# Gated recurrent heads in pairs on the free axis, and the level of 64 spread over both column halves

## The chip, the cores and the metric

The kernel runs on one core of a Trainium2 chip. The metric is the time of one execution on the device, in microseconds (us); lower is better. The core's engines are TensorE (PE in the profile; PEld is its weight load), VectorE (DVE), ScalarE (ACT), GpSimd (POOL) and SyncE (SP, whose queue issues most DMAs).

## The reference, cut to what matters

The program is three layers on a sequence of S = 512 positions and D = 1024 channels: first a block with its own mixers and a feed-forward part (`first_block`), then two layers of `hybrid_layer`. The change concerns the recurrence in those two, `hgrn2`: 8 heads of width 128, in chunks.

```python
def hgrn2(q, f_logit, i, lb):
    # S_t = diag(f_t) S_{t-1} + (1 - f_t) i_t^T,  o_t = S_t^T q_t
    ...
    qf = silu(q)
    logf = logaddexp(log(max(lb, LB_FLOOR)), log1p(-lb) + log_sigmoid(f_logit))
    k = -expm1(logf)
    ...
    def step(state, xs):
        qch, kch, vch, b = xs          # b = cumulative sum of logf in the chunk
        decay = exp(b_t - b_s) for s <= t, else 0
        scores = einsum('bhtd,bhsd,bhtsd->bhts', qch, kch, decay)
        o = scores @ vch + (qch * exp(b)) @ state
        state = exp(b_last) * state + (kch * exp(b_last - b))^T @ vch
        return state, o

def hybrid_layer(x, w_in, w_out, g_pre, g_post, lb, g_head, sinks):
    proj = rms_norm(x, g_pre) @ w_in
    q_h, f_h, i_h, z_h, q_a, k_a, v_a, z_a = split(proj)
    o_h = rms_norm(hgrn2(q_h, f_h, i_h, lb), g_head) * silu(z_h)
    o_a = sliding_window_attention(rotary(q_a), rotary(k_a), v_a, sinks) * silu(z_a)
    return x + rms_norm(concat(o_h, o_a) @ w_out, g_post)
```

## The kernel before, in words

**Order of the work.** The code is written with a scheduler that places each instruction on its engine's queue by a priority: without more, the order of the text. `K.above(mark)` gives a piece of code a priority above what follows the mark, `EVP` puts the copies out of the accumulators ahead of these, and `prio=20000` the splitting of weights ahead of all. The queue of each engine is fixed when the program is built; on the chip each engine goes through its own queue in order.

**Projections.** `gemm_a` and `gemm_b` multiply the layer's input with 512 columns of weights. Each float32 product is made from three (L149, L150, L151): both operands are split into a high and a low part, ACT casting the high part of the weights (L137) and DVE subtracting (L138). Eight row blocks times three make 24 matmuls for one accumulator `mm`, of which there are two. A callback `evac` takes the accumulator out.

**Tags.** A tile is asked for by a tag with so many buffers; a new tile of that tag waits until the one before it in its buffer has had its last reader. `ev` (4) holds what the evacuations need for a short time: the sigmoid in `proj_q`, `proj_zh` and `proj_za`, two tiles of the rotary evacuation (`rope`, L522 to L524), and one more in `turn` of `proj_kv`. `ha` (4) and `hb` (4) serve the attention, `f` (4) the gates, `zs` (2) the output gates read back. In the accumulator memory (PSUM) the tags `xa` and `xb` have two banks each, `xc` one; heads and attention share them.

**A head** (`hgrn`, L413 to L511) takes three 128x512 tiles with the head's 128 channels on the partitions and time on the free axis: q, k and the decay f. It builds the masked score matrix from the diagonal outwards in 7 levels, b = 1, 2, 4, ... 64. At each level PE multiplies blocks of k with blocks of q, and DVE's masked copies (L435, L436, L445, L452) or ACT's copies (L456, L465, L471) put the part that belongs to this level into a matrix `C` and then `ST`. Then DVE scales (L478, L479) the later half of q's blocks and the earlier half of k's by the decay products of the neighbouring block, which are in T, and multiplies neighbours in T (L481) to get the products for blocks twice as long. So a level's matmuls need the scaling of the level before, and overwriting q and k needs the matmuls of the level.

The matmuls of a level contract over all 128 partitions. Up to b = 32 they have 32 columns of weights, and `pa[32 * j:32 * j + 32, ...]` puts the outputs on four groups of 32 rows in turn (at b = 32 two groups): 16, 16, 16, 16, 16, 8 matmuls. At b = 64 there are four with 64 columns of weights, all on rows 0 to 63:

```python
for c in range(NT):
    o = c * P
    nc.tensor.matmul(pb[0:64, 64 * c:64 * c + 64], k[:, o:o + 64], q[:, o + 64:o + 128])
nc.scalar.copy(ST[0:64, :, 64:128], pb[0:64, 0:256].rearrange("p (c t) -> p c t", c=4))
```

Level 1 reads q through a copy `qx` (L421, L423) of 16 blocks of 48 columns. Levels b = 1, 2, 4 use the bank `pa` (tag `xa`), the others `pb` (tag `xb`). After the levels the head transposes k (L486), forms the states of the chunks (L490 to L494), and the output from `ST` and the states (L498, L500), normalises it (L504 to L510) and multiplies it with its output gate, all through the one bank of `xc`.

**The layer** runs projections of the first four heads (`proj_i`, `proj_q`, `proj_f`), then heads 0 to 3 with priority over the next projections, `proj_kv`, `proj_zh`, `proj_qa`, `proj_za`, then heads 4 to 7 in the same way, then the attention in eight `swa_pair` calls, whose last ones have the first half of the output projection (`wo1`) behind them; `wo2` needs all attention results. Two layers of 8 heads are 16 heads.

Of the kernel before, what the change touches and what calls it, by code (L numbers as in the profile page):

```python
# [8 lines left out]
F32 = mybir.dt.float32  # L9
# [3 lines left out]
AF = mybir.ActivationFunctionType  # L13
ALU = mybir.AluOpType
# [3 lines left out]
P = 128  # L18
S = 512
D = 1024  # L20
NT = S // P
KT = D // P
EPS = 1e-6
# [295 lines left out]
def layer(K, l, xd, win, wout, gpost, lbp, ghead, sinks, out, gnext):  # L319

    nc, tc = K.nc, K.tc
    if True:
        def page(tag, bufs):
            return K.lp.tile([P, S], F32, name=K.nm("pg"), tag=tag, bufs=bufs)

        def ev():
            return page("ev", 4)

        def ha():
            return page("ha", 4)  # L330

        def hb():
            return page("hb", 4)
# [36 lines left out]
        def proj_q(c):  # L370
            quad = K.quad()

            def evac(m, ps):
                h = 4 * c + m
                sg = ev()
                nc.scalar.activation(sg, ps, AF.Sigmoid)
                q = quad[:, m, :]
                nc.vector.scalar_tensor_tensor(q, ps, om[:, h:h + 1], sg, ALU.mult, ALU.mult)
                qh[h] = q
            K.gemm_a(win[:, c * S:(c + 1) * S], evac)  # L380

        def proj_f(c):
            quad = K.quad()

            def evac(m, ps):
                h = 4 * c + m
                k, f = quad[:, m, :], page("f", 4)
# [3 lines left out]
                fh[h] = (f, k)  # L391
            K.gemm_a(win[:, D + c * S:D + (c + 1) * S], evac)
# [20 lines left out]
        def hgrn(h):  # L413
            q, (f, k) = qh.pop(h), fh.pop(h)
            v = vh[h // 4]
            vc = slice((h % 4) * P, (h % 4 + 1) * P)
            ST, C = K.STs[h % 2], K.Cs[h % 2]
            zs = page("zs", 2).rearrange("p (c d) -> p c d", c=NT)
            nc.sync.dma_start(out=zs, in_=zh_d[:, h * P:(h + 1) * P].rearrange("(c p) d -> p c d", p=P))
            qx = K.lp.tile([P, 16, 48], F32, name=K.nm("qx"), tag="qx", bufs=1)  # L420
            nc.scalar.copy(qx[:, :, 0:32], q.rearrange("p (n t) -> p n t", n=16))  # L421
            nc.vector.tensor_tensor(q, q, f, ALU.mult)
            nc.scalar.copy(qx[:, :, 32:48], q.rearrange("p (n t two) -> p n t two", n=16, two=2)[:, :, :, 1])  # L423
            pa, pb = K.psum("xa"), K.psum("xb")
            T, b = f, 1
            Cf = C.rearrange("p c t -> p (c t)")
            for lev in range(7):
                if b == 1:
                    for c in range(NT):
                        for j in range(4):  # L430
                            o = c * P + 32 * j
                            nc.tensor.matmul(pa[32 * j:32 * j + 32, 48 * c:48 * c + 48], k[:, o:o + 32], qx[:, 4 * c + j, :])
                    p1 = pa[:, 0:192].rearrange("p (c t) -> p c t", c=NT)
                    m1 = K.hgmask[:, 0:192]
                    nc.vector.copy_predicated(C, m1[:, 0:P].rearrange("p (c t) -> p c t", c=NT), p1[:, :, 0:32])  # L435
                    nc.vector.copy_predicated(C.rearrange("p c (t two) -> p c t two", two=2)[:, :, :, 1],  # L436
                                              m1[:, P:192].rearrange("p (c t) -> p c t", c=NT), p1[:, :, 32:48])
                elif b <= 8:
                    pl, o0 = (pb, 320) if b == 8 else (pa, 64 + P * lev)
                    for c in range(NT):  # L440
                        for j in range(4):
                            o = c * P + 32 * j
                            nc.tensor.matmul(pl[32 * j:32 * j + 32, o0 + 32 * c:o0 + 32 * c + 32],
                                             k[:, o:o + 32], q[:, o:o + 32])
                    nc.vector.copy_predicated(Cf, K.hgmask[:, 64 + P * lev:64 + P * (lev + 1)], pl[:, o0:o0 + P])  # L445
                elif b == 16:
                    for c in range(NT):
                        for j in range(4):
                            o = c * P + 32 * j
                            nc.tensor.matmul(pb[32 * j:32 * j + 32, 256 + 16 * c:272 + 16 * c],  # L450
                                             k[:, o:o + 32], q[:, o + 16:o + 32])
                    nc.vector.copy_predicated(C[:, :, 16:32], K.hgmask[:, 576:640].rearrange("p (c t) -> p c t", c=4),  # L452
                                              pb[:, 256:320].rearrange("p (c t) -> p c t", c=4))
                    for j in range(4):
                        r = slice(32 * j, 32 * j + 32)
                        nc.scalar.copy(ST[r, :, r], C[r, :, :])  # L456
                elif b == 32:
                    for c in range(NT):
                        for j in range(2):
                            o = c * P + 64 * j  # L460
                            nc.tensor.matmul(pb[64 + 32 * j:96 + 32 * j, 32 * c:32 * c + 32],
                                             k[:, o:o + 32], q[:, o + 32:o + 64])
                    for j in range(2):
                        r = slice(64 * j, 64 * j + 32)
                        nc.scalar.copy(ST[r, :, 64 * j + 32:64 * j + 64],  # L465
                                       pb[64 + 32 * j:96 + 32 * j, 0:P].rearrange("p (c t) -> p c t", c=4))
                else:
                    for c in range(NT):
                        o = c * P
                        nc.tensor.matmul(pb[0:64, 64 * c:64 * c + 64], k[:, o:o + 64], q[:, o + 64:o + 128])  # L470
                    nc.scalar.copy(ST[0:64, :, 64:128], pb[0:64, 0:256].rearrange("p (c t) -> p c t", c=4))  # L471
                n = S // (2 * b)
# [7 lines left out]
                T2 = K.lc.tile([P, n], F32, name=K.nm("T"), tag=f"T{n}", bufs=1 if n >= 128 else 2)  # L480
                nc.vector.tensor_tensor(T2, T4[:, :, 0], T4[:, :, 1], ALU.mult)  # L481
                T, b = T2, 2 * b
            pk = K.psum("xc", 1).rearrange("p (c d) -> p c d", c=NT)
            kt = hb().rearrange("p (c d) -> p c d", c=NT)
            for c in range(NT - 1):
                nc.tensor.transpose(pk[:, c, :], k[:, c * P:(c + 1) * P], K.ident)  # L486
            nc.scalar.copy(kt[:, 0:3, :], pk[:, 0:3, :])
            pS = K.psum("xc", 1).rearrange("p (c d) -> p c d", c=NT)
            for c in range(NT - 1):
                nc.tensor.matmul(pS[:, c, :], kt[:, c, :], v[c][:, vc])  # L490
            Ss = hb().rearrange("p (c d) -> p c d", c=NT)
            nc.vector.tensor_copy(Ss[:, 0, :], pS[:, 0, :])
            for c in range(1, NT - 1):
                nc.vector.scalar_tensor_tensor(Ss[:, c, :], Ss[:, c - 1, :], T[:, c:c + 1], pS[:, c, :],  # L494
                                               ALU.mult, ALU.add)
            po = K.psum("xc", 1).rearrange("p (c d) -> p c d", c=NT)
            for c in range(NT):
                nc.tensor.matmul(po[:, c, :], ST[:, c, :], v[c][:, vc], start=True, stop=(c == 0))  # L498
                if c:
                    nc.tensor.matmul(po[:, c, :], q[:, c * P:(c + 1) * P], Ss[:, c - 1, :], start=False, stop=True)  # L500
            o = page("on", 8).rearrange("p (c d) -> p c d", c=NT)
            ss = K.small(NT, "hss", 4)
            for c in range(NT):
                nc.scalar.activation(kt[:, c, :], po[:, c, :], AF.Square, accum_out=ss[:, c:c + 1])  # L504
            nc.vector.tensor_tensor(o, po, zs, ALU.mult)
            ms = K.small(NT, "hms", 4)
            nc.vector.tensor_scalar(ms, ss, 1.0 / P, EPS, ALU.mult, ALU.add)  # L507
            rs = K.rsqrt(ms)
            for c in range(NT):
                nc.vector.tensor_scalar(o[:, c, :], o[:, c, :], rs[:, c:c + 1], None, ALU.mult)  # L510
            on[h] = o  # L511
# [69 lines left out]
        oa = [page("f", 4) for _ in range(4)] + [page("on", 8) for _ in range(4)]  # L581
# [70 lines left out]
        with K.above(p0):  # L652
            for h in range(4):
                hgrn(h)
# [4 lines left out]
        with K.above(p1):  # L659
            for h in range(4, 8):  # L660
                hgrn(h)
# [606 lines left out]
```

## Time and profile before

| | |
|---|---|
| runs | 1810.46, 1810.53 and 2941.12 us, median 1810.53 us |
| profiled execution | 1814.22 us, span of its instructions 1812.5 us |
| granted TensorE clock, mean | 0.993 |
| PE busy | 98% of the span |
| DVE busy, ACT busy, POOL busy | 60%, 48%, 10% |
| instructions on PE, DVE | 11600, 2186 |

Busy is the time in which at least one instruction of the engine is under way; matmuls overlap, and their ends are modelled, so that 98% is an upper reading of how full PE is. Start times count from the span's start. The two layers with heads run from about 840 to 1338 us and from there to the end.

### The profile page before, as it was taken

How to read it: one execution, taken by the hardware profiler on the slowest of the kernel's cores; microseconds unless marked ns; L12 is line 12 of the kernel's file. 1: busy time of each engine (PE TensorE's matmuls, PEld its weight loads, DVE VectorE, ACT ScalarE, POOL GpSimd, SP SyncE). 2: the span in 40 equal slices, each digit the busy share in tenths (PEclk: the TensorE clock that was granted, in tenths of full speed). 3: DMA queues.
4: the chain of work that ended last, by engine and by line, in shares of the span. 5: the costliest groups of instructions: out<-in, count | busy, mean ns of one | idle time of the engine just before them, and what ended most of it. 6: DMA issues, size and time to landing. Idle time of an engine off the chain costs nothing.

```text
span 1812.5 us, 29438 instructions
## 1 busy us (share of the span) xinstructions
PE 1775.7 (98%) x11600; PEld 1460.7 (81%) x11600; DVE 1080.5 (60%) x2186; ACT 864.0 (48%) x1707; POOL 172.6 (10%) x231
## 2 busy tenths in 40 slices
PE   7999999999899999999999999999999999999998
PEld 5878887787698888878888888878878888888886
DVE  4375445557455665588474666766364748577744
ACT  4457744344343443445443445766343334376741
POOL 1001111010000110012000001100120000111002
PEclk9999999999999999999999999999999999999999
DMA  7342433121623847388322233332342322332222
GB/s 211 75 109 80 90 93 93 47 93 47 197 94 101 236 114 189 94 205 235 109 88 84 88 100 100 100 110 82 108 154 88 112 76 65 119 127 76 82 70 93
DMA packets 114322, 201.05 MB, mean 111 GB/s; under 512 B 9600, under 2 KB 20224, under 8 KB 114184
## 3 DMA queue, kind: packets, MB, share of 16 engines
q1 hardware_dynamic: 105480, 182.40, 32.6%
q0 software_dynamic: 8704, 16.78, 5.3%
q8 instruction: 91, 1.49, 0.3%
q14 instruction: 47, 0.39, 0.1%
HBM read 184.45 MB, written 14.70 MB: 110 GB/s over the span
## 4 chain that ended last, share of the span: by engine, by line
PE 92%; DMA 3%; ACT 2%; DVE 1%; issue 1%; POOL 0%; SPq 0%; DVEq 0%; POOLq 0%; ACTq 0%
PE mm L150 23%; PE mm L151 23%; PE mm L149 23%; PE xc L638 2%; PE xa L602 2%; PE xa L228 2%; PE xa L227 2%; PE xa L229 2%; PE mm L227 1%; PE mm L228 1%; PE mm L229 1%; PE xc L1069 1%; PE xa L1051 1%; PE xb L624 1%; PE xc L498 1%; DMA wr<-in_w_in_dram 1%
## 5 line engine op out<-in xcount | busy, mean ns | idle before, releaser
L149 PE MATMUL mm<-wh,hh 128*128 128x512 f32 (+1 forms) x896 | 350.0, 391 | 9.5 <-ACT hh L258 3.7
L138 DVE TENSOR_TENSOR wl<-wr,wh 128x1024 fp32r<-128x1024 f32 (+1 forms) x240 | 288.5, 1211 | 114.4 <-PE mm L150 70.8
L150 PE MATMUL mm<-wl,hh 128*128 128x512 f32 (+1 forms) x896 | 350.0, 391 | 0.8 <-DVE wl L138 0.8
L151 PE MATMUL mm<-wh,hl 128*128 128x512 f32 (+1 forms) x896 | 349.1, 393 | 0.0
L137 ACT CAST wh<-wr 128x1024 fp32r<-128x1024 f32 (+1 forms) x240 | 246.6, 1038 | 118.6 <-PE mm L151 55.3
L149 PE MATMUL mm<-hh,wh 128*128 128x512 f32 x640 | 253.6, 396 | 1.4 <-ACT pg L803 1.4
L151 PE MATMUL mm<-hh,wl 128*128 128x512 f32 x640 | 252.3, 394 | 2.1 <-DVE wl L138 2.0
L150 PE MATMUL mm<-hl,wh 128*128 128x512 f32 x640 | 252.3, 394 | 0.0
L149 PEld LDWEIGHTS mm<-wh,hh 128*128 128x128 f32 x896 | 170.5, 190 | 43.6 <-ACT hh L258 4.3
L150 PEld LDWEIGHTS mm<-wl,hh 128*128 128x128 f32 x896 | 170.4, 190 | 34.7 <-DVE wl L138 2.4
L151 PEld LDWEIGHTS mm<-wh,hl 128*128 128x128 f32 x896 | 169.1, 190 | 31.5 <-DVE hl L259 0.5
L151 PEld LDWEIGHTS mm<-hh,wl 128*128 128x128 f32 x640 | 120.3, 188 | 28.4 <-DVE wl L138 3.3
L149 PEld LDWEIGHTS mm<-hh,wh 128*128 128x128 f32 x640 | 120.2, 188 | 28.1 <-ACT pg L803 2.7
L150 PEld LDWEIGHTS mm<-hl,wh 128*128 128x128 f32 x640 | 120.4, 188 | 24.5 <-issue 0.2
L115 POOL TENSOR_TENSOR sm<-sm,nhalf 128x4 f32<-128x4 f32 (+1 forms) x64 | 59.0, 922 | 491.6 <-DVE sm L507 331.4
L149 PE MATMUL mm<-qd,wh 128*128 128x512 f32 (+1 forms) x288 | 105.5, 366 | 0.0
L150 PE MATMUL mm<-qd,wh 128*128 128x512 f32 (+1 forms) x288 | 105.4, 366 | 0.0
L151 PE MATMUL mm<-qd,wl 128*128 128x512 f32 (+1 forms) x288 | 105.2, 365 | 0.0
L610 ACT ACTIVATE pg<-pg,sm 128x256 f32<-128x256 f32 (+1 forms) x128 | 60.9, 478 | 11.0 <-DVE sm L608 10.6
L1151 DVE TENSOR_TENSOR hr<-hr 128x512 f32<-128x512 f32 (+1 forms) x36 | 22.7, 631 | 69.4 <-ACT hr L1150 68.8
L151 PEld LDWEIGHTS mm<-qd,wl 128*128 128x128 f32 x288 | 54.3, 189 | 8.8
L149 PEld LDWEIGHTS mm<-qd,wh 128*128 128x128 f32 x288 | 54.3, 189 | 8.8
(311 smaller groups left out, 2996.9 us busy)
## 6 DMA issues: line engine op xcount, KB each, us to landing
wr<-in_w_in_dram SPq DMA_DIRECT2D x160, 512.0 KB, 4.9
wr<-in_w_out_dram SPq DMA_DIRECT2D x40, 512.0 KB, 3.5
wr<-in_w_up_dram SPq DMA_DIRECT2D x32, 512.0 KB, 5.7
wr<-in_w_down_dram SPq DMA_DIRECT2D x32, 512.0 KB, 5.9
wx<-in_w_down_dram POOLq DMA_DIRECT2D x24, 512.0 KB, 9.5
wx<-in_w_down_dram SPq DMA_DIRECT2D x8, 512.0 KB, 3.5
wr<-in_w_down_dram POOLq DMA_DIRECT2D x8, 512.0 KB, 8.4
zh<-pg SPq DMA_DIRECT2D x16, 256.0 KB, 2.5
```

What stands on the lines that cost most here:

```text
L115: self.nc.gpsimd.tensor_tensor(y, ms, e, ALU.pow)
L137: nc.scalar.copy(hi, raw)
L138: nc.vector.tensor_tensor(lo, raw, hi.bitcast(F32), ALU.subtract)
L149: nc.tensor.matmul(ps, sh, mh, start=(k == 0), stop=False)
L150: nc.tensor.matmul(ps, sh, ml, start=False, stop=False)
L151: nc.tensor.matmul(ps, sl, mh, start=False, stop=(k == n - 1))
L227: nc.tensor.matmul(ps, ah, wh, start=(first and k == 0), **kw)
L228: nc.tensor.matmul(ps, ah, wl, start=False, **kw)
L229: nc.tensor.matmul(ps, al, wh, start=False, **kw)
L602: nc.tensor.matmul(psc[:, i, 2 * P - wi:], qT[p][e][:, t1 - P:t1], kT[kv][j][:, t1 - wi:t1], start=(j == 0), stop=(j == 1))
L610: nc.scalar.activation(prw, prw, AF.Exp, bias=pn[:, n:n + 1], scale=-1.0, accum_out=den[:, n:n + 1])
L638: nc.tensor.matmul(o, va[0][:, k, vv], pTs[e][k // 2][:, k % 2, w], start=(k == n), stop=(k < n or n == 0))
```

## The change

`hgrn(h)` becomes `hgrn2(i)` for heads 2i and 2i + 1. Their q, k and f lie side by side in 1024 columns, so that one DVE instruction scales both; matmuls, masked copies and everything after the levels are still done for each head (`for e in range(2)`), with both heads' matmuls of a level ahead of both heads' copies. A pair takes two banks of `xa` and two of `xb`. The first decay product, now of 512 columns, is a tile of tag `ev`; `f` is two tiles of 1024 columns (`f2`), `ha` too (`ha2`, handed out in halves by `ha`), and `qx` uses `ha2`. The smaller decay products have one buffer each. At b = 64 the four matmuls of a head go to rows 0 to 63 and 64 to 127 in turn, and two copies of half the width take them to `ST`.

```diff
+        half = []
+        def ha2():
+            return K.lp.tile([P, 2 * S], F32, name=K.nm("pg"), tag="ha", bufs=2)
         def ha():
-            return page("ha", 4)
+            if half:
+                return half.pop()
+            t = ha2()
+            half.append(t[:, S:])
+            return t[:, :S]
+        def f2():
+            return K.lp.tile([P, 2 * S], F32, name=K.nm("pg"), tag="f", bufs=2)
...
-        def hgrn(h):
-            q, (f, k) = qh.pop(h), fh.pop(h)
+        def hgrn2(i):
+            q, (f, k) = qh.pop(i), fh.pop(i)
...
+            W = 2 * S
+            zs, qx, pa, pb = [], [], [], []
+            for e in range(2):
+                zs.append(page("zs", 2).rearrange("p (c d) -> p c d", c=NT))
+                h = 2 * i + e
+                nc.sync.dma_start(out=zs[e], in_=zh_d[:, h * P:(h + 1) * P].rearrange("(c p) d -> p c d", p=P))
+                qx.append(ha2()[:, :768].rearrange("p (n t) -> p n t", t=48))
+                nc.scalar.copy(qx[e][:, :, 0:32], q[:, e * S:e * S + S].rearrange("p (n t) -> p n t", n=16))
             nc.vector.tensor_tensor(q, q, f, ALU.mult)
...
             for lev in range(7):
+                for e in range(2):
                     for c in range(NT):
                         for j in range(4):
+                            o = e * S + c * P + 32 * j
...
+                    if b == 64:
+                        for c in (0, 2, 1, 3):
+                            o = e * S + c * P
+                            r, w = slice(c // 2 * 64, c // 2 * 64 + 64), slice(128 + c % 2 * 64, 192 + c % 2 * 64)
+                            nc.tensor.matmul(pb[e][r, w], k[:, o:o + 64], q[:, o + 64:o + 128])
+                for e in range(2):
...
+                    else:
+                        for j in range(2):
+                            nc.scalar.copy(ST[0:64, 2 * j:2 * j + 2, 64:128],
+                                           pb[e][64 * j:64 * j + 64, 128:256].rearrange("p (c t) -> p c t", c=2))
-                n = S // (2 * b)
+                n = W // (2 * b)
...
                 nc.vector.tensor_tensor(q4[:, :, 1, :], q4[:, :, 1, :], te, ALU.mult)
                 nc.vector.tensor_tensor(k4[:, :, 0, :], k4[:, :, 0, :], to, ALU.mult)
-                T2 = K.lc.tile([P, n], F32, name=K.nm("T"), tag=f"T{n}", bufs=1 if n >= 128 else 2)
+                T2 = ev() if n == S else K.lc.tile([P, n], F32, name=K.nm("T"), tag=f"T{n}", bufs=1)
...
+            for e in range(2):
+                ST = K.STs[e]
...
-        oa = [page("f", 4) for _ in range(4)] + [page("on", 8) for _ in range(4)]
+        oa = [t[:, j * S:(j + 1) * S] for t in (f2(), f2()) for j in range(2)] + [page("on", 8) for _ in range(4)]
...
-            for h in range(4):
-                hgrn(h)
+            for i in range(2):
+                hgrn2(i)
```

## Rows read from the trace of the kernel before

**Rows 1.** Page, busy us (share of the span) and instructions of each engine.
```profile
PE 1775.7 (98%) x11600; PEld 1460.7 (81%) x11600; DVE 1080.5 (60%) x2186; ACT 864.0 (48%) x1707; POOL 172.6 (10%) x231
```
**Rows 2.** Windows: length, busy PE, PEld, DVE, ACT, POOL (count), PE clock, DMA share, GB/s.
```profile
1040.00:1060.00 20.00, 20.00 (x375) 17.10 (x363) 19.08 (x60) 11.09 (x27) 1.70 (x3) 1.00 0.15 40
```
**Rows 3.** Waits of PE, whole run: total us, times, longest us.
```profile
PE xa L602 <- DVE sm L608: 1.4, 2, 0.7
```
**Rows 4.** Timeline of PE about one burst: start us, us until the last end, instruction, count.
```profile
921.40 0.39 PE L149 MATMUL mm<-wh,hh 128*128 128x512 f32 x1
921.63 0.39 PE L150 MATMUL mm<-wl,hh 128*128 128x512 f32 x1
921.95 0.76 PE L443 MATMUL xa<-qd,qd 128*32 128x32 f32 x64
922.64 0.50 PE L151 MATMUL mm<-wh,hl 128*128 128x512 f32 x1
922.98 0.40 PE L149 MATMUL mm<-wh,hh 128*128 128x512 f32 x1
```
**Rows 5.** Timeline of PE, a short burst of the same line.
```profile
1048.98 0.26 PE L443 MATMUL xa<-qd,qd 128*32 128x32 f32 x6
1049.17 0.39 PE L151 MATMUL mm<-wh,hl 128*128 128x256 f32 x1
```
**Rows 6.** Timeline of PE, the level of 32 of one head.
```profile
1047.08 0.45 PE L461 MATMUL xb<-qd,qd 128*32 128x32 f32 x16
1047.46 0.39 PE L150 MATMUL mm<-wl,hh 128*128 128x256 f32 x1
```
**Rows 7.** Timeline of PE, the level of 64 of one head.
```profile
1045.33 0.68 PE L470 MATMUL xb<-qd,qd 128*64 128x64 f32 x8
1045.93 0.39 PE L151 MATMUL mm<-wh,hl 128*128 128x256 f32 x1
```
**Rows 8.** Timeline of PE, the first and the last of the bursts.
```profile
909.82 0.55 PE L432 MATMUL xa<-qx,qd 128*32 128x48 f32 x32
...
1600.79 0.33 PE L470 MATMUL xb<-qd,qd 128*64 128x64 f32 x2
```
**Rows 9.** Timeline of PE in the attention: full-width transposes, then halves of 64.
```profile
1157.74 0.27 PE L626 MATMUL xb<-ident,pg 128*128 128x128 f32 x1
1157.85 0.27 PE L624 MATMUL xb<-ident,pg 128*128 128x128 f32 x1
1158.05 1.75 PE L638 MATMUL xc<-pg,pg 128*64 128x128 f32 x28
1159.73 0.73 PE L602 MATMUL xa<-qd,qd 128*128 128x128 f32 x4
```
**Rows 10.** Instruction groups of ACT: count, busy us, mean ns, idle us before.
```profile
L471 ACT COPY ST<-xb 64x256 f32<-64x256 f32 x16 | 5.9, 367 | 18.0 <-PE xb L470 18.0
```
**Rows 11.** Instruction groups of DVE, in the same columns.
```profile
L479 DVE TENSOR_TENSOR qd<-qd,T 128x256 f32<-128x256 f32 x96 | 40.7, 424 | 0.0
L422 DVE TENSOR_TENSOR qd<-qd,pg 128x512 f32<-128x512 f32 x16 | 11.0, 688 | 0.1
L481 DVE TENSOR_TENSOR T<-pg 128x256 f32<-128x256 f32 x16 | 6.7, 417 | 0.0
L481 DVE TENSOR_TENSOR T<-T 128x32 f32<-128x32 f32 (+5 forms) x96 | 19.0, 201 | 1.4
```
**Rows 12.** Timeline: last attention result, last copy of the first output projection.
```profile
1258.88 0.69 DVE L640 TENSOR_TENSOR pg<-xc,pg 128x512 f32<-128x512 f32 x1 [0.62 <-PE xc L638]
...
1281.89 0.58 ACT L690 COPY pg<-mm 128x512 f32<-128x512 f32 x1
```
**Rows 13.** Timeline of DVE: first head's first decay product and its last reader.
```profile
904.72 0.42 DVE L481 TENSOR_TENSOR T<-pg 128x256 f32<-128x256 f32 x1
...
917.52 0.42 DVE L479 TENSOR_TENSOR qd<-qd,T 128x256 f32<-128x256 f32 x1
```

More of the change, by code (lines that the diff above doesn't have):

```diff
@@ L377, in evac @@
                 q = quad[:, m, :]
+                qh[h // 2] = quad[:, m // 2 * 2:m // 2 * 2 + 2, :].rearrange("p h t -> p (h t)")
                 nc.vector.scalar_tensor_tensor(q, ps, om[:, h:h + 1], sg, ALU.mult, ALU.mult)
-                qh[h] = q
             K.gemm_a(win[:, c * S:(c + 1) * S], evac)
@@ L386, in evac @@
                 h = 4 * c + m
-                k, f = quad[:, m, :], page("f", 4)
+                if m % 2 == 0:
+                    fh[h // 2] = (f2(), quad[:, m:m + 2, :].rearrange("p h t -> p (h t)"))
+                k, f = quad[:, m, :], fh[h // 2][0][:, m % 2 * S:m % 2 * S + S]
                 nc.scalar.activation(f, ps, AF.Sigmoid)
@@ L390, in evac @@
                 nc.vector.tensor_scalar(f, f, om[:, h:h + 1], fl[:, h:h + 1], ALU.mult, ALU.add)
-                fh[h] = (f, k)
             K.gemm_a(win[:, D + c * S:D + (c + 1) * S], evac)
@@ L411, in layer @@
         on = {}
-        def hgrn(h):
-            q, (f, k) = qh.pop(h), fh.pop(h)
[L415 to L421, printed above, removed]
-            nc.vector.tensor_tensor(q, q, f, ALU.mult)
-            nc.scalar.copy(qx[:, :, 32:48], q.rearrange("p (n t two) -> p n t two", n=16, two=2)[:, :, :, 1])
-            pa, pb = K.psum("xa"), K.psum("xb")
+        def hgrn2(i):
+            q, (f, k) = qh.pop(i), fh.pop(i)
+            v = vh[i // 2]
+            W = 2 * S
[6 more added lines that the diff above has]
+                nc.scalar.copy(qx[e][:, :, 0:32], q[:, e * S:e * S + S].rearrange("p (n t) -> p n t", n=16))
+            nc.vector.tensor_tensor(q, q, f, ALU.mult)
+            for e in range(2):
+                nc.scalar.copy(qx[e][:, :, 32:48],
+                               q[:, e * S:e * S + S].rearrange("p (n t two) -> p n t two", n=16, two=2)[:, :, :, 1])
+                pa.append(K.psum("xa"))
+                pb.append(K.psum("xb"))
@@ L425, in hgrn @@
             T, b = f, 1
-            Cf = C.rearrange("p c t -> p (c t)")
             for lev in range(7):
-                if b == 1:
+                for e in range(2):
                     for c in range(NT):
                         for j in range(4):
[L431 to L440, printed above, removed]
-                        for j in range(4):
[L442 to L458, printed above, removed]
-                        for j in range(2):
[L460 to L471, printed above, removed]
-                n = S // (2 * b)
@@ new lines, in hgrn2 @@
+                            o = e * S + c * P + 32 * j
+                            r = slice(32 * j, 32 * j + 32)
+                            if b == 1:
+                                nc.tensor.matmul(pa[e][r, 48 * c:48 * c + 48], k[:, o:o + 32], qx[e][:, 4 * c + j, :])
+                            elif b <= 8:
+                                pl, o0 = (pb[e], 320) if b == 8 else (pa[e], 64 + P * lev)
+                                nc.tensor.matmul(pl[r, o0 + 32 * c:o0 + 32 * c + 32], k[:, o:o + 32], q[:, o:o + 32])
+                            elif b == 16:
+                                nc.tensor.matmul(pb[e][r, 256 + 16 * c:272 + 16 * c], k[:, o:o + 32], q[:, o + 16:o + 32])
+                            elif b == 32 and j % 2 == 0:
+                                nc.tensor.matmul(pb[e][64 + 16 * j:96 + 16 * j, 32 * c:32 * c + 32],
+                                                 k[:, o:o + 32], q[:, o + 32:o + 64])
@@ new lines, in hgrn2 @@
+                    if b == 64:
[4 more added lines that the diff above has]
+                for e in range(2):
+                    ST, C = K.STs[e], K.Cs[e]
+                    Cf = C.rearrange("p c t -> p (c t)")
+                    if b == 1:
+                        p1 = pa[e][:, 0:192].rearrange("p (c t) -> p c t", c=NT)
+                        m1 = K.hgmask[:, 0:192]
+                        nc.vector.copy_predicated(C, m1[:, 0:P].rearrange("p (c t) -> p c t", c=NT), p1[:, :, 0:32])
+                        nc.vector.copy_predicated(C.rearrange("p c (t two) -> p c t two", two=2)[:, :, :, 1],
+                                                  m1[:, P:192].rearrange("p (c t) -> p c t", c=NT), p1[:, :, 32:48])
+                    elif b <= 8:
+                        pl, o0 = (pb[e], 320) if b == 8 else (pa[e], 64 + P * lev)
+                        nc.vector.copy_predicated(Cf, K.hgmask[:, 64 + P * lev:64 + P * (lev + 1)], pl[:, o0:o0 + P])
+                    elif b == 16:
+                        nc.vector.copy_predicated(C[:, :, 16:32], K.hgmask[:, 576:640].rearrange("p (c t) -> p c t", c=4),
+                                                  pb[e][:, 256:320].rearrange("p (c t) -> p c t", c=4))
+                        for j in range(4):
+                            r = slice(32 * j, 32 * j + 32)
+                            nc.scalar.copy(ST[r, :, r], C[r, :, :])
+                    elif b == 32:
+                        for j in range(2):
+                            r = slice(64 * j, 64 * j + 32)
+                            nc.scalar.copy(ST[r, :, 64 * j + 32:64 * j + 64],
+                                           pb[e][64 + 32 * j:96 + 32 * j, 0:P].rearrange("p (c t) -> p c t", c=4))
+                    else:
+                        for j in range(2):
+                            nc.scalar.copy(ST[0:64, 2 * j:2 * j + 2, 64:128],
+                                           pb[e][64 * j:64 * j + 64, 128:256].rearrange("p (c t) -> p c t", c=2))
@@ L485, in hgrn @@
[L485 to L511, printed above, removed]
+            for e in range(2):
+                ST = K.STs[e]
+                h, o1 = 2 * i + e, e * S
+                vc = slice((h % 4) * P, (h % 4 + 1) * P)
+                pk = K.psum("xc", 1).rearrange("p (c d) -> p c d", c=NT)
+                kt = hb().rearrange("p (c d) -> p c d", c=NT)
+                for c in range(NT - 1):
+                    nc.tensor.transpose(pk[:, c, :], k[:, o1 + c * P:o1 + (c + 1) * P], K.ident)
+                nc.scalar.copy(kt[:, 0:3, :], pk[:, 0:3, :])
+                pS = K.psum("xc", 1).rearrange("p (c d) -> p c d", c=NT)
+                for c in range(NT - 1):
+                    nc.tensor.matmul(pS[:, c, :], kt[:, c, :], v[c][:, vc])
+                Ss = hb().rearrange("p (c d) -> p c d", c=NT)
+                nc.vector.tensor_copy(Ss[:, 0, :], pS[:, 0, :])
+                for c in range(1, NT - 1):
+                    nc.vector.scalar_tensor_tensor(Ss[:, c, :], Ss[:, c - 1, :], T[:, 4 * e + c:4 * e + c + 1], pS[:, c, :],
+                                                   ALU.mult, ALU.add)
+                po = K.psum("xc", 1).rearrange("p (c d) -> p c d", c=NT)
+                for c in range(NT):
+                    nc.tensor.matmul(po[:, c, :], ST[:, c, :], v[c][:, vc], start=True, stop=(c == 0))
+                    if c:
+                        nc.tensor.matmul(po[:, c, :], q[:, o1 + c * P:o1 + (c + 1) * P], Ss[:, c - 1, :], start=False, stop=True)
+                o = page("on", 8).rearrange("p (c d) -> p c d", c=NT)
+                ss = K.small(NT, "hss", 4)
+                for c in range(NT):
+                    nc.scalar.activation(kt[:, c, :], po[:, c, :], AF.Square, accum_out=ss[:, c:c + 1])
+                nc.vector.tensor_tensor(o, po, zs[e], ALU.mult)
+                ms = K.small(NT, "hms", 4)
+                nc.vector.tensor_scalar(ms, ss, 1.0 / P, EPS, ALU.mult, ALU.add)
+                rs = K.rsqrt(ms)
+                for c in range(NT):
+                    nc.vector.tensor_scalar(o[:, c, :], o[:, c, :], rs[:, c:c + 1], None, ALU.mult)
+                on[h] = o
@@ L659, in layer @@
         with K.above(p1):
-            for h in range(4, 8):
-                hgrn(h)
+            for i in range(2, 4):
+                hgrn2(i)
         p2 = mark()
```

2 lines of the change are left out of this document (removed).

## The prediction

> **What bounds the kernel now.** I start with the engines' busy shares: TensorE (PE) is busy for 1775.7 of 1812.5 us, VectorE (DVE) for 1080.5 [rows 1]. A busy PE is not yet a limit, so the second view is the stretches in which the recurrent heads run: from 1040 to 1060 us, where DVE is fullest (19.08 of 20), PE is busy for all 20.00 us at a granted clock of 1.00 [rows 2]. Third, who PE waits for: of the stages of `layer` the longest entry is L602 in the attention, 1.4 us in the whole run, and no matmul of `hgrn` (L432 to L470) is in the list [rows 3]. So in this part the time is the sum of what PE issues, back to back, and the change is worth what it takes off PE's own issue time. Work saved on DVE and ScalarE (ACT) counts only where PE would wait for it.
>
> PE's issue time is read from starts, not from durations, since matmuls overlap: a 128x512 matmul lasts 0.39 us, but the next one starts 0.23 us later (921.40, 921.63) [rows 4]. The small matmuls of the recurrence come as bursts between those of the projections. I take three readings of such a burst.
>
> First, its length. 64 rows of L443 occupy 0.69 us (921.95 to 922.64), 6 rows 0.19 us (1048.98 to 1049.17) [rows 4, 5]: 0.50 us for 58, so 8.6 ns each and a fixed 0.14 us at the end. (One float32 matmul of the code is two instructions here; "rows" counts the instructions.)
>
> Second, what a burst costs beyond its own matmuls. From the last large matmul ahead of those 64 (921.63) to the second one after (922.98) it is 1.35 us [rows 4]. Two large slots of 0.23 are 0.46, the 64 are 64 x 8.6 ns = 0.55; 0.34 us remain. That is the price of going from full-width to 32-column matmuls and back, whatever the burst holds.
>
> Third, column groups. L443 uses all four groups of 32 columns in turn and needs 8.6 ns a row. L461 uses two of them: (0.38 - 0.14)/16 = 15 ns [rows 6]. L470, the level of 64, writes all its outputs to rows 0 to 63, one column half: (0.60 - 0.14)/8 = 58 ns [rows 7].
>
> There are 80 such bursts in the run (40 in each layer, the same in both), the first at 909.82, the last at 1600.79 [rows 8]. The code asks for 7 a head (one a level), 112 for 16 heads; that they are 80 says that the order already puts levels of different heads together, though it also splits a few.
>
> **The change part by part.**
>
> *Level of 64 in both halves.* The four matmuls of a head now go alternately to rows 0 to 63 and 64 to 127. The nearest row is L638, which alternates halves of 64 with streams of 128: 28 rows from 1158.05 to 1159.73, (1.68 - 0.14)/28 = 55 ns, where full-width ones of the same stream need 110 (1157.74, 1157.85) [rows 9]. Halves taken in turn run at twice the rate; the step from four groups to two (8.6 to 15 ns) says the same. So 58 becomes some 29 ns: 8 x 29 ns = 0.23 us a head, 3.7 us for 16 heads. Bounds: nothing, and 58 down to L461's 15 ns, 5.5 us. I take 3.7, as L638 has halves of the same width. On ACT one copy of 64x256 becomes two of half the size, which cost no more than 0.37 us each, the price of the whole [rows 10]: at most 16 x 0.37 = 5.9 us more, hidden, as ACT is busy for 11.09 of 20 us there [rows 2].
>
> The Trainium skill (TensorE: Matmul & The Clock Gate, Part 3: Packing small matmuls) says that a weight load overlaps running matmuls only where the row groups differ. All of these matmuls contract over 128 rows, so by it neighbours in other column halves would gain nothing, and this term would be 0. The rates of L461 and L638 speak against it.
>
> *Heads in pairs.* The matmuls are the same in number and size. What changes is that both heads' matmuls of a level become ready together, since one DVE scaling serves both: 7 levels x 8 pairs = 56 bursts if each level of a pair is one burst. 24 fewer than 80, times 0.34 us, are 8.2 us. Bounds: if two pairs overlap as heads do now, by the present ratio 80/112, 56 becomes 40, and 40 fewer are 13.6 us; if the two heads' groups are issued apart and nothing merges, 112 bursts, 32 more, lose 10.9 us. I take 56: a pair holds all four banks of the tags xa and xb, so a second pair can begin only once the first has copied its third level out of xa, which leaves little to merge across pairs.
>
> *DVE.* Per level two heads' scalings of 128x256 (0.42 us; 112 of L479, 96 of them in the row, and as many of L478) become half as many of 128x512, priced as L422's 0.69 us [rows 11]: 224 x 0.423 = 94.8 to 112 x 0.688 = 77.1, minus 17.7 us. The decay products (L481) take 6.7 + 19.0 = 25.7 us; half of that and 8 new ones of 512 columns at 0.69 are 18.4: minus 7.3. Together 25 us of 1080. I cost this at nothing in time: PE does not wait for DVE here [rows 2, 3]. Were that cover gone, the place would be 1040 to 1060, and there fewer DVE instructions would help.
>
> *Buffers.* The staging copy qx moves from its own tile to the tag ha, now two tiles of 1024 columns; f likewise is now two tiles. ha's only other users in the heads' time are the attention pairs, which come later and find it coarser (a tile comes free only as a whole). Cost taken as 0; the cover is the projection wo1 behind the attention: the last attention result is written at 1258.88, the last copy of wo1 at 1281.89 [rows 12], so 23 us of PE work are in hand if the attention ends later. The 512-column decay product is placed in the tag ev, which the evacuations of the projections use; taken as 0, see the rivals. The loads of zs are issued for both heads at once on SP's queue and wait for two free tiles, as a second and third head's do now; what queues behind them is weight loads, which are issued a whole projection ahead.
>
> Sum: -3.7 - 8.2 = -11.9 us. The profiled execution took 1814.22 us, of which 1.7 lie around the span; it would take 1802.3. The median of the runs is 1810.53, 3.7 less; on that scale 1798.6.
>
> **The rivals.**
>
> *No fewer bursts* (80 as now): the present order merges heads already, and two pairs in flight hold no more work than two or three heads. Only the level of 64 remains: 1810.5 - 3.7 = 1806.8. For it: 80 where 112 are asked for. Against: 56 needs no luck, only that equal work ready together is issued together.
>
> *The alternation gains nothing* (the rule above): -8.2, 1802.3. For it: no row shows L470 itself in two halves; against it, L461 and L638.
>
> *More merging* (44 bursts): -3.7 - 36 x 0.34 = -15.9, 1794.6. For it: xa comes free after the third level, so the last levels of one pair can meet the first of the next.
>
> *Slower: an evacuation waits for a tile of ev.* The first 256-wide product is made at 904.72 and read until 917.52 + 0.42 [rows 13], 13 us; its successor would hold one of four tiles of ev about as long. The rotary evacuations (L522 to L524) hold up to three, in the key-value projection four. An evacuation that waits leaves PE one more bank of the projection, 24 matmuls of half width at half of 0.23 us, 2.9 us, and as much in the one in work; 13 - 5.8 = 7 us of idle PE. Once in each layer, 14 us: 1812.6; for two pairs in each layer, 28 us: 1826.6. It decides from 11.9 us of idle PE on, 6 a layer. Against it: the tiles of one evacuation are mostly back before the next, since heads' bursts spread these evacuations, and DVE has fewer instructions in front.
>
> **How the numbers follow.** The forecast (-12, within 3 us) gets 0.55, no fewer bursts 0.17, no gain from alternation 0.10, more merging 0.08, slower 0.10. Predicted 1798.6 us. The range runs from 1791 (more merging with the alternation's far bound, 5.5, and 2 us to spare) to 1812 (no fewer bursts and no gain, and a little of the wait for ev); beyond it lie most of the slower rival and the case of 112 bursts, 1817.7. 2% is 36 us, about what a measurement of this kernel can tell from no change. Downwards no case reaches it: with no price of any burst left (80 x 0.34 = 27.2 us) and the far bound of the alternation it would be 32.7; 0.01. Slower by as much needs the wait for ev at more than three pairs in each layer; 0.02. Within 2%: 0.97.
>
> **What would show it.** Right: rows of the level of 64 at some 29 ns where 58 stand now; bursts of 128 rows for one level of a pair (64 a head); fewer than 70 bursts; DVE some 25 us less busy with no change in PE's waits. Wrong: waits of PE for an evacuation that itself waits on a tile of ev, bursts of single heads, or an idle PE between 900 and 1130 us.

## The result: slower, and the profile after

The changed kernel takes 1853.17 us (median of 4 runs, 1849.35 to 1856.56), the kernel before on the same chip 1811.79. The ratio is 1.023, with an interval of 1.0203 to 1.0258: slower, by some 41 us, where 12 us less had been forecast. The profiled execution took 1849.35 us, its span 1847.6.

The engines' busy shares of the changed kernel, in the columns of [rows 1]:

```profile
PE 1784.1 (97%) x11600; PEld 1466.3 (79%) x11600; DVE 1076.0 (58%) x2010; ACT 855.0 (46%) x1715; POOL 177.8 (10%) x231
```

PE is idle for 1847.6 - 1784.1 = 63.5 us, before for 1812.5 - 1775.7 = 36.8 [rows 1]: 26.7 us more. The mean granted clock fell from 0.993 to 0.986; (1 - clock) x span is 25.9 us now and 12.7 before, so up to 13.2 us more went to the lower clock (less than that, as clock lost while PE is idle costs nothing). Together up to 39.9 us, against 35.1 us of longer span and the few us that the change saves. So it isn't more work; PE ran dry, and ran at half clock around these places. The windows tell where. Of the changed kernel (columns as in [rows 2]):

```profile
940.00:980.00 40.00, 40.00 (x178) 33.14 (x177) 9.49 (x10) 10.51 (x15) 0.00 (x0) 1.00 0.33 105
...
1060.00:1080.00 20.00, 17.29 (x85) 14.06 (x84) 7.72 (x19) 3.71 (x13) 2.28 (x2) 0.93 0.29 102
...
1180.00:1200.00 20.00, 10.75 (x61) 8.91 (x60) 9.49 (x33) 10.68 (x41) 2.01 (x2) 0.74 0.28 94
1200.00:1220.00 20.00, 18.26 (x150) 15.30 (x149) 17.59 (x67) 16.23 (x56) 1.01 (x1) 0.92 0.15 41
```

The same stretches of the kernel before:

```profile
940.00:980.00 40.00, 40.00 (x465) 32.98 (x464) 26.42 (x71) 16.55 (x37) 1.03 (x1) 1.00 0.33 100
...
1180.00:1200.00 20.00, 20.00 (x134) 16.23 (x133) 9.67 (x18) 8.29 (x19) 1.29 (x1) 1.00 0.23 78
1200.00:1220.00 20.00, 18.65 (x107) 15.44 (x106) 15.27 (x45) 15.34 (x36) 0.00 (x0) 1.00 0.43 145
```

Two things are to be seen. From 940 to 980 us PE is full in both, but with 178 matmuls where 465 stood: only projections, no heads, and DVE works for 9.49 of 40 us. From 1180 to 1200 us PE, which was full, is busy for 10.75 of 20 at a granted clock of 0.74, which mixes the two levels, 2.4 and 1.2 GHz. (A smaller gap comes before: 2.7 us of idle PE from 1060 to 1080.) The heads left the first place and are late in the second. What PE waits for (waits of the whole run, as [rows 3]; two waits of L286 aside, far from the heads, 10.7 us now and 10.9 before) are now the stages of a head:

```profile
PE xc L511 <- DVE pg L530: 6.2, 4, 2.0
PE xc L515 <- ACT pg L512: 4.9, 6, 1.0
PE xb L465 <- ACT ST L487: 4.9, 2, 2.4
PE xc L523 <- DVE pg L519: 4.6, 2, 2.3
```

These are the chain of one head (level of 32 copied out, level of 64, transposes of k, states, output, gate), which no other work covers any longer. The last head's gate (L530) and the last evacuation of the projection ahead of the attention (L600) show why. The last three gates, in DVE's timeline:

```profile
1182.92 0.69 DVE L530 TENSOR_TENSOR pg<-xc,pg 128x512 f32<-128x512 f32 x1 [2.28 <-ACT pg L529]
...
1195.89 0.69 DVE L530 TENSOR_TENSOR pg<-xc,pg 128x512 f32<-128x512 f32 x1 [3.81 <-ACT pg L529]
...
1206.73 0.69 DVE L530 TENSOR_TENSOR pg<-xc,pg 128x512 f32<-128x512 f32 x1
```

Before, the last one (L505 there) ran at

```profile
1153.74 0.69 DVE L505 TENSOR_TENSOR pg<-xc,pg 128x512 f32<-128x512 f32 x1
```

The last sigmoid of that projection moved the other way: in ACT's timeline, before (as L575) and now:

```profile
1208.33 0.59 ACT L575 ACTIVATE pg<-mm 128x512 f32<-128x512 f32 x1
```

```profile
1179.32 0.60 ACT L600 ACTIVATE pg<-mm 128x512 f32<-128x512 f32 x1
```

So the projections, which are the filler, are used up 29 us earlier, and the heads that needed them beside them end 53 us later. What made them late stands in DVE's timeline, from the first pair's product of q and the decay (L438) to the first decay product (L502, now in a tile of `ev`, shown as pg):

```profile
908.34 1.22 DVE L438 TENSOR_TENSOR qd<-qd,pg 128x1024 f32<-128x1024 f32 x1
...
985.89 1.29 DVE L502 TENSOR_TENSOR pg<-pg 128x512 f32<-128x512 f32 x2
...
987.75 0.68 DVE L499 TENSOR_TENSOR qd<-qd,pg 128x512 f32<-128x512 f32 x1
988.35 0.68 DVE L500 TENSOR_TENSOR qd<-qd,pg 128x512 f32<-128x512 f32 x1
...
1118.59 1.29 DVE L502 TENSOR_TENSOR pg<-pg 128x512 f32<-128x512 f32 x2
```

The product needs f alone, which L438 read at 908.34. It runs 78 us later, for the first two pairs at once, and the next two pairs' run at 1118.59, again together. Before, it ran at 904.72 [rows 13]. In the text of `layer`, heads 0 to 3 stand behind `proj_zh(0)`, `proj_i(1)`, `proj_q(1)` and `proj_f(1)`, and heads 4 to 7 behind `proj_kv`, `proj_zh(1)`, `proj_qa(0)` and `proj_za(0)`; `K.above` gives the heads the priority over these. ACT's timeline has, just ahead of each, the last sigmoid that takes a tile of `ev` in a projection that stands ahead of the heads in the text (L388 in the second `proj_q`, L600 in the first `proj_za`):

```profile
985.52 0.59 ACT L388 ACTIVATE pg<-mm 128x512 f32<-128x512 f32 x1
...
1117.32 0.60 ACT L600 ACTIVATE pg<-mm 128x512 f32<-128x512 f32 x1
```

No row of waits names the product: what is late is its place in DVE's queue, which is fixed when the program is built. The second of the two layers shows the same (products at 1484.36 and 1615.94).

### The profile page after: what moved, and what is told of

Read it like the earlier page. It is cut to its first block, busy times and chain, and to the rows that moved or that the text cites. A ratio compares the mean times of both kernels' runs of the same rounds, so it can differ in the third digit from the quotient of the medians.

```text
span 1847.6 us, 29272 instructions
## 1 busy us (share of the span) xinstructions
PE 1784.1 (97%) x11600; PEld 1466.3 (79%) x11600; DVE 1076.0 (58%) x2010; ACT 855.0 (46%) x1715; POOL 177.8 (10%) x231
## 4 chain that ended last, share of the span: by engine, by line
PE 88%; DVE 4%; ACT 4%; DMA 3%; issue 1%; SPq 0%; POOL 0%; DVEq 0%; POOLq 0%; ACTq 0%
PE mm L149 22%; PE mm L150 22%; PE mm L151 22%; PE xa L227 2%; PE xa L228 1%; PE xa L229 1%; PE xc L663 1%; PE xa L627 1%; PE mm L227 1%; PE mm L229 1%; PE mm L228 1%; PE xc L1094 1%; PE xa L1076 1%; PE xc L523 1%; ACT pg L635 1%
## 5 line engine op out<-in xcount | busy, mean ns | idle before, releaser
L115 POOL TENSOR_TENSOR sm<-sm,nhalf 128x4 f32<-128x4 f32 (+1 forms) x64 | 64.7, 1012 | 314.0 <-DVE sm L532 191.3
L549 POOL TENSOR_TENSOR pg<-pg,pg 128x512 f32<-128x512 f32 (+1 forms) x24 | 28.1, 1172 | 447.8 <-DVE pg L548 439.9
L635 ACT ACTIVATE pg<-pg,sm 128x256 f32<-128x256 f32 (+1 forms) x128 | 60.7, 479 | 7.1 <-DVE sm L633 6.9
```

The lines of the kernel that those rows point to most:

```text
L115: self.nc.gpsimd.tensor_tensor(y, ms, e, ALU.pow)
L549: nc.gpsimd.tensor_tensor(dst, dst, a, ALU.add)
L635: nc.scalar.activation(prw, prw, AF.Exp, bias=pn[:, n:n + 1], scale=-1.0, accum_out=den[:, n:n + 1])
```

## The experiments

Three explanations stood against each other. *Order*: tiles of the tag `ev` are given out in the order of the text, so a head's product comes behind the evacuations of projections that stand ahead of it in the text, although the heads have priority over these. *Full*: `ev` is short of tiles. *Pairing*: two heads at a time, with all banks of `xa` and `xb`, are late by themselves.

**An own tile for the product** (the changed kernel with one line altered):

```diff
-                T2 = ev() if n == S else K.lc.tile([P, n], F32, name=K.nm("T"), tag=f"T{n}", bufs=1)
+                T2 = K.lc.tile([P, n], F32, name=K.nm("T"), tag=f"T{n}", bufs=1)
```

> The changed kernel with one edit: the 512-column decay product gets a tile of its own in place of one of the tag ev. Theory A (ev is handed out in the order of the text, so the product waits behind the evacuations of the projections that stand ahead of the heads in the text): the head pairs start their second level at 910 to 930 us again, PE does not run dry at 1180 us, and the time is 1795 to 1805 us. Theory B (ev is full when the product asks for it): the same time. Theory C (the pairing itself, with all banks of xa and xb taken by one pair, postpones the heads): 1845 us or more, as now.

Measured: 1802.47 us (5 runs, 1801.74 to 1804.47), the kernel before 1812.99 beside it, ratio 0.994 (0.9927 to 0.9954). The whole loss is gone, and this version is faster than both kernels. Its page and two of its windows:

```profile
PE 1763.2 (98%) x11600; PEld 1451.1 (81%) x11600; DVE 1072.4 (60%) x2010; ACT 873.9 (49%) x1731; POOL 173.1 (10%) x231
```
```profile
940.00:980.00 40.00, 40.00 (x539) 32.42 (x528) 25.12 (x52) 18.65 (x45) 1.53 (x1) 1.00 0.38 117
...
1180.00:1200.00 20.00, 20.00 (x135) 16.32 (x136) 10.70 (x28) 11.97 (x26) 0.00 (x0) 1.00 0.22 78
```

Heads fill 940 to 980 again, and PE is full at full clock from 1180 to 1200. Pairing as such postpones nothing. Of the 46.6 us between the spans (1847.6 and 1801.0), half falls in each layer: the second layer's first L438 runs at 1406.81 there and at 1383.48 here, 23.3 us apart.

**The same product put into `ev` in the kernel before**, single heads, nothing else changed:

```diff
-                T2 = K.lc.tile([P, n], F32, name=K.nm("T"), tag=f"T{n}", bufs=1 if n >= 128 else 2)
+                T2 = ev()[:, :n] if n == 256 else K.lc.tile([P, n], F32, name=K.nm("T"), tag=f"T{n}", bufs=1 if n >= 128 else 2)
```

> The kernel before, heads one by one, with one edit: its first decay product (256 columns) is a tile of ev. Theory A: the single heads wait as the pairs do; 1840 to 1870 us. Theory B: four heads' products compete with the evacuations; somewhere between 1811 and 1850. Theory C: the place of this product doesn't matter; 1811 within 4 us.

Measured: 1849.41 us (4 runs), ratio 1.0199 (1.0186 to 1.0213). The products of four heads in DVE's timeline, and a window:

```profile
985.18 1.09 DVE L481 TENSOR_TENSOR pg<-pg 128x256 f32<-128x256 f32 x3
...
988.39 0.42 DVE L481 TENSOR_TENSOR pg<-pg 128x256 f32<-128x256 f32 x1
```
```profile
1180.00:1200.00 20.00, 12.65 (x70) 10.89 (x69) 11.34 (x33) 13.57 (x42) 2.01 (x2) 0.75 0.40 126
```

One line in the old kernel costs 36 us where the whole change lost 41, at the same two places. The loss is the tile, with or without pairs.

**Five tiles of `ev`** in the changed kernel (`return page("ev", 5)` for `page("ev", 4)`):

> The changed kernel with five tiles of the tag ev in place of four. Theory A (tiles are given in the order of the text): the product still waits for the last sigmoid of the projection ahead of it in the text, near 986 and 1118 us in the first layer with heads; 1845 to 1858 us. Theory B (ev is full): a free fifth tile lets the product run near 910 us; 1800 to 1815 us.

Measured: 1846.14 us, ratio 1.0178 (1.0161 to 1.0194). The product still runs at

```profile
986.29 1.29 DVE L502 TENSOR_TENSOR pg<-pg 128x512 f32<-128x512 f32 x2
```

still behind the same sigmoid (985.93). A shortage of tiles is not what holds it up: *full* falls as the cause. The fifth tile took off some 7 us by the times (1846.14 for 1853.17) and 9 by the ratios; of the loss of 51 us, a shortage explains that much at most.

**The tile asked for earlier**: `th[h // 2] = ev()` in `proj_f`, ahead of the projections in question; the product is written where it was.

```diff
+                    th[h // 2] = ev()
...
-                T2 = ev() if n == S else K.lc.tile(...)
+                T2 = th.pop(i) if n == S else K.lc.tile(...)
```

> The changed kernel with the product still in ev, four tiles, but the tile is asked for in the text of the gate projection that fills the pair's f, ahead of the evacuations that stood before it. Theory A: the product runs near 910 us and the time is that of the run with the product's own tile, 1799 to 1810 us. Theory B: ev has as many users as before; 1845 us or more.

Measured: 1854.4 us, ratio 1.0227 (1.0209 to 1.0244), products at

```profile
984.89 1.29 DVE L503 TENSOR_TENSOR pg<-pg 128x512 f32<-128x512 f32 x2
...
1119.12 1.29 DVE L503 TENSOR_TENSOR pg<-pg 128x512 f32<-128x512 f32 x2
```

A miss for *order* as I had put it: where the tile is asked for changes nothing. What this kernel left where it was is the first instruction that writes the tile. So the theory was restated: the order of the first writes in the text counts. The traces bear it out beyond this run: in all six kernels with products that are written in the head and lie in `ev`, the first product of each group starts 0.3 to 1.3 us after the start of the last sigmoid of `proj_q(1)` or `proj_za(0)`.

**The product written earlier**: the same, but the multiplication itself also stands in `proj_f`, behind the second f of a pair, and the head takes it from `th`; `ev` keeps its four tiles.

```diff
+                if m % 2:
+                    th[h // 2] = ev()
+                    f4 = fh[h // 2][0].rearrange("p (n two) -> p n two", two=2)
+                    nc.vector.tensor_tensor(th[h // 2], f4[:, :, 0], f4[:, :, 1], ALU.mult)
```

> The changed kernel with the first decay product of a pair (512 columns, in a tile of the tag ev, still 4 tiles) computed where f's second evacuation of the pair is written, so that its first write stands ahead, in the text, of the evacuations of the projections that follow. Nothing else moves and ev keeps its four tiles. If what counts is the order in which the first writes into tiles of ev stand in the text: the products run near 910 us, ahead of the last sigmoid of the second q projection, and the time is that of the kernel with an own tile, 1799 to 1808 us. If any place in ev is late or ev is short of tiles: the products are late still, or the projections now wait for the tiles that the products keep, and the time is 1845 us or more. Between, 1810 to 1840 us: the order is mended but the tiles kept by the products hold projections up.

Measured: 1802.44 us (4 runs, 1802.04 to 1803.09), ratio 0.9946 (0.9929 to 0.9963), the time of the own tile. The products run beside their f:

```profile
907.91 0.69 DVE L408 TENSOR_TENSOR pg<-pg 128x512 f32<-128x512 f32 x1
...
920.56 0.69 DVE L408 TENSOR_TENSOR pg<-pg 128x512 f32<-128x512 f32 x1
```

Same tag, same four tiles, and no loss: the place in the text of the first write decides. The multiplication moved with the write, but its own place is not what counts: with an own tile it stands in the head and is on time. Holding tiles of `ev` until the heads have read them costs nothing that can be measured here (1802.44 us for 1802.47 with the own tile). Why the scheduler serves a tag in this order, no run here shows.

**Which half of the heads costs how much.** `ev` for the last two pairs of each layer only (`ev() if n == S and i >= 2 else ...`), and for the first two only (`i < 2`):

> The changed kernel with the product's own tile for the first two pairs of a layer and ev for the last two. Theory A: heads 0 to 3 run at 910 to 990 us, heads 4 to 7 still begin at 1118 us; if the price is paid where PE runs dry with the attention at 1180 us, this stays slow, 1830 to 1848 us.

> The reverse: ev for the first two pairs of a layer, the product's own tile for the last two. Theory A: heads 0 to 3 begin at 986 us, heads 4 to 7 follow them directly instead of waiting until 1118, and end before the attention; if lateness costs nothing while projections are left to fill PE, 1800 to 1815 us.

Measured: last two 1832.48 us, ratio 1.0103 (1.0087 to 1.012); first two 1820.02, ratio 1.0033 (1.002 to 1.0047). The second is above what was expected of it. Against the own tile that is 30.0 and 17.6 us, and both together, as in the changed kernel, about 51. PE's busy time in the two, last and first:

```profile
PE 1774.1 (97%) x11600; PEld 1460.4 (80%) x11600; DVE 1074.1 (59%) x2010; ACT 853.0 (47%) x1715; POOL 175.3 (10%) x231
```
```profile
PE 1771.8 (97%) x11600; PEld 1459.8 (80%) x11600; DVE 1073.0 (59%) x2010; ACT 876.8 (48%) x1731; POOL 178.9 (10%) x231
```

With spans of 1829.7 and 1817.5 us PE is idle for 55.6 and 45.7, that is 17.8 and 7.9 more than with the own tile (1801.0 - 1763.2 = 37.8). The sum, 25.7, is what the changed kernel has more (63.5 - 37.8). The last two pairs cost more. That less projection is left behind them to fill PE fits this; it was not tested apart.

**The two gains, each alone.** The level of 64 in both halves, in the kernel before:

```diff
-                    for c in range(NT):
+                    for c in (0, 2, 1, 3):
...
-                        nc.tensor.matmul(pb[0:64, 64 * c:64 * c + 64], k[:, o:o + 64], q[:, o + 64:o + 128])
-                    nc.scalar.copy(ST[0:64, :, 64:128], pb[0:64, 0:256].rearrange("p (c t) -> p c t", c=4))
+                        r, w = slice(c // 2 * 64, c // 2 * 64 + 64), slice(128 + c % 2 * 64, 192 + c % 2 * 64)
+                        nc.tensor.matmul(pb[r, w], k[:, o:o + 64], q[:, o + 64:o + 128])
+                    for j in range(2):
+                        nc.scalar.copy(ST[0:64, 2 * j:2 * j + 2, 64:128],
+                                       pb[64 * j:64 * j + 64, 128:256].rearrange("p (c t) -> p c t", c=2))
```

> The kernel before with the level of 64 alone changed: alternately into both column halves, two copies. By the rate of L638: 58 to 29 ns a row, 3.7 us less, 1807 to 1808 us, and the rows of the level of 64 alone read 29 to 32 ns. If neighbours in other column halves don't overlap: 1811 us and 58 ns.

Measured: 1805.89 us (5 runs), ratio 0.996 (0.9948 to 0.9973). PE's timeline at one head's level of 64 (the line below it is what PE starts next):

```profile
943.37 0.45 PE L471 MATMUL xb<-qd,qd 128*64 128x64 f32 x8
943.75 0.35 PE L461 MATMUL xb<-qd,qd 128*32 128x32 f32 x10
```

The 8 rows take 0.38 us where they took 0.60 [rows 7]: (0.38 - 0.14)/8 = 30 ns a row for 58.

And pairs with an own tile, but the level of 64 put back into one half:

```diff
-                        for c in (0, 2, 1, 3):
+                        for c in range(NT):
...
-                            nc.tensor.matmul(pb[e][r, w], k[:, o:o + 64], q[:, o + 64:o + 128])
+                            nc.tensor.matmul(pb[e][0:64, 64 * c:64 * c + 64], k[:, o:o + 64], q[:, o + 64:o + 128])
```

> As the run with the product's own tile, but the level of 64 is put back: four matmuls of a head into one column half, one copy. If the alternation is worth what the rows of L638 say (29 ns in place of 58 a row), this is 3 to 4 us slower than the run before it (theories A and B: 1799 to 1809 us); if alternation gains nothing, equal to it within 1 us.

Measured: 1809.46 us (11 runs), ratio 0.998 (0.9971 to 0.9989). The 16 rows of a pair, and what follows:

```profile
954.32 1.15 PE L464 MATMUL xb<-qd,qd 128*64 128x64 f32 x16
955.39 0.76 PE L455 MATMUL xa<-qd,qd 128*32 128x32 f32 x64
```

Here (1.07 - 0.14)/16 = 58 ns. With the alternation, in the kernel with the own tile, it is

```profile
952.16 0.69 PE L465 MATMUL xb<-qd,qd 128*64 128x64 f32 x16
952.78 0.50 PE L149 MATMUL mm<-wh,hh 128*128 128x512 f32 x1
```

30 ns. So the four kernels stand, against the kernel before (1812.99): alternation alone -7.1 us, pairs alone -3.5, both -10.5. The alternation was expected to be worth 3 to 4 us in either place. It gained 7.1 alone and 7.0 on top of pairs (1809.46 to 1802.47): both expectations miss.

What do all bursts of the levels take in PE's timeline? Count each from the start of the last other matmul ahead of it to the start of the second one after it, less what these two neighbours take elsewhere (medians: 0.227 us for 128x512, 0.120 for 128x256, 0.109 for 128x128). The sums are 63.6 us before, 57.0 with the alternation, 60.7 with pairs and 53.7 with both: minus 6.6, 2.9 and 9.9. Each difference in time is thus found again in these bursts, to within 0.6 us. In the 60.7 of pairs alone, 1.7 us are two waits of PE for DVE (0.89 and 0.76) and not matmuls.

## Why the prediction was wrong

**What bounds the kernel.** Right for the kernel before, and not enough. PE was full and waited for no head because DVE got each head's levels done early enough to lie among the projections. That order is itself a resource, and nothing in the busy shares shows how much of it is left.

**The step that failed** is in the part on buffers: "The 512-column decay product is placed in the tag ev, which the evacuations of the projections use; taken as 0". It is worth some 51 us (1853.2 against 1802.5). The slower rival had the right tag with the wait the wrong way round: it let an evacuation wait for a tile that a product holds, 13 us, and reached 1826.6 at most. What happened is that the product, and with it every level from the second on, came behind the evacuations. Four tiles of `ev` were free enough, as the kernels with five tiles and with the product in `proj_f` show. What I did not ask is in which order a shared tag serves its users when their priority and their place in the text differ. [rows 13] had the number to ask it with: the product at 904.72, ahead of whole projections that stand ahead of it in the text.

**How 78 us of delay became 41.** The delay itself cost nothing at first: from 940 to 980 PE was full with projections. Most of the bill came at 1180, when these were used up. "An idle PE between 900 and 1130 us" was named as a sign of error. A little of it showed there (2.7 us from 1060 to 1080); the larger part, 9.25 us, came 50 us later than that.

**The level of 64.** The rate was right, the size too small. A row went from 58 to 30 ns (29 forecast), 8 x 28 ns x 16 = 3.6 us. The rival that gave this term 0 falls. The runs do not agree with what the prediction drew for it from the rule of the Trainium skill (TensorE: Matmul & The Clock Gate, Part 3: Packing small matmuls): float32 matmuls in alternate column halves take 30 ns a row for 58. But 7.1 us came for 3.7. All rows of this level, each run of them counted to the start of the next other matmul, take 11.2 us before and 6.9 with the alternation, with pairs 9.7 and 5.5: 4.2 less both times. The rest goes, alone, with ten bursts fewer (80 to 70), and on top of pairs with the two waits that are gone (1.7 us) and two bursts fewer. Why the order of the bursts changed so was not tried.

**Pairs.** The mechanism was right, the size not: 8.2 us forecast, 3.5 measured alone. The mis-sized step is "56 bursts if each level of a pair is one burst". With an own tile there are 68 (one half: 70), from these causes, counted in PE's timeline: 56, less 6 where a level of the next pair joined, and 18 more, of which 14 are bursts cut by 128-wide transposes or products of finished heads and of the rotary step, and 4 are second heads of a pair whose level of 64 came by itself. The price per burst comes out at (63.6 - 60.7)/10 = 0.29 us, or 0.46 with the two waits of PE taken out of the 60.7; 0.34 was forecast. One sign was misread: "bursts of 128 rows for one level of a pair (64 a head)" cannot come, as 16 matmuls of a head are 32 rows; a pair's level is 64.

**The sum.** Without the failed step it comes near: -10.5 us measured with the own tile, -11.9 forecast. In part that is luck: pairs gave 4.7 us less than forecast and the alternation 3.3 to 3.4 more, and the two misses offset each other.

**DVE.** 25 us less were forecast, 4.5 came (1080.5 to 1076.0), with no effect on time, as forecast. Durations had been added up, and they overlap: in the rows of DVE above, two 512-column scalings of 0.68 us start 0.60 apart (987.75, 988.35). Counted from each start to the next one, scalings, decay products and the products of q and f take 108.9 us before and 99.7 now, 9.2 less; the rest of DVE's work shows 4.4 more, and the runs give no cause for that. Costs of a queue are to be taken from starts, as was done for PE.

## What to carry to other kernels

Where a tile moves to a shared tag, ask not only whether the tag has enough buffers, but where its first write stands in the text among the tag's other users: code that a scheduler runs ahead by priority can be held back to its place in the text by one tile. A delay that shows no wait and no idle engine where it happens can be paid for much later, where the filler is used up; look for it in the counts of instructions in windows, not in the waits. And a saving of a few us is measured only once such a step is separated out: one line with its own tile turned 41 us of loss into 10 of gain.

## What the runs showed of the hardware

Idle time of PE came with a lower clock behind it. In the changed kernel the stretch from 1180 to 1200 us, in which PE is idle for 9.25 us, has a granted clock of 0.74, between the two levels of 2.4 and 1.2 GHz: 1.00 from 1190 to 1193, 0.50 from 1194 to 1200. In the timeline of PE there the same products double in price after a wait:

```profile
1192.14 0.71 PE L523 MATMUL xc<-qd,ST 128*128 128x128 f32 x4 [2.32 <-DVE pg L519]
1192.69 0.39 PE L525 MATMUL xc<-pg,qd 128*128 128x128 f32 x2
1192.91 0.42 PE L523 MATMUL xc<-qd,ST 128*128 128x128 f32 x2
1193.13 0.63 PE L525 MATMUL xc<-pg,qd 128*128 128x128 f32 x2
1193.56 0.63 PE L523 MATMUL xc<-qd,ST 128*128 128x128 f32 x2
```

Two of them take 0.22 us (1192.69 to 1192.91) and from 1193.13 on 0.43. Waits of 2 us are thus paid for beyond their own length. This is part of why a chain of short waits cost so much here: by the estimate from the mean clocks above, up to 13.2 us.
